# A hybrid attention layer on one core: fox scores and values as two free streams, memory tiles loaded ahead, decode preparation in four steps

## Chip, cores and metric

The program runs on one core of a Trainium2 chip. The metric is the device time of one execution in microseconds (us). TensorE (PE) does the matmuls and transposes, VectorE (DVE), ScalarE (ACT) and GpSimd (POOL) the rest; SyncE (SP) issues every DMA.

## The reference, cut to what matters

One layer over a prompt of 2048 tokens (D 1024) and 8 decode streams of 16 tokens with caches of 2048. A projection of the normalised input feeds three branches: forgetting attention ("fox", 8 heads of 64), retention (4 heads), and cross-attention to 256 memory tokens (4 heads of 128). Each is gated, projected, merged, and goes through one output projection. The change concerns fox and memory attention:

```python
def fox_attend(q, c_q, q_pos, k, v, c_k):
    s = jnp.einsum('bqhd,bkhd->bhqk', q, k) * (DH_FOX ** -0.5)
    s = s + c_q[..., :, None] - c_k[..., None, :]      # (axes swapped to heads first)
    s = jnp.where(k_pos[None, :] <= q_pos[:, None], s, -jnp.inf)
    p = jax.nn.softmax(s, axis=-1).astype(v.dtype)
    return jnp.einsum('bhqk,bkhd->bqhd', p, v)
...
def memory_attend(q, mk, mv):
    s = jnp.einsum('bthd,bmhd->bhtm', q, mk.astype(q.dtype), preferred_element_type=jnp.float32) * (DH_MEM ** -0.5)
    p = jax.nn.softmax(s, axis=-1).astype(q.dtype)
    return jnp.einsum('bhtm,bmhd->bthd', p, mv.astype(q.dtype))
```

For the prompt c is the running sum of log f, k_pos up to the query's own; for the decode the queries see the cached keys (with the sums of the cached log f taken from the end) and their own 16.

## The kernel before, in words

The program first runs the projection of all tokens (up to 1683 us), then a **weave** of two lanes, then out blocks 1 to 4.

- The right lane runs retention and then `fox` (L1252): 64 units (h, b), a head and a block of 256 queries. `scores(h, b)` goes through chunks of 512 keys, twice each (128 queries at a time): matmuls into a PSUM tile sc (L1290, L1291, the mask L1293; there are two sc banks), a maximum on DVE (L1297), the exponential on ACT into a tile pt (L1298). At the unit's end the factors f_nm of the softmax are worked out on DVE (L1218 to L1226) and POOL scales every pt (L1302). `values(h, b)` transposes pt (L1324), splits each transpose into a high part ph (ACT, L202) and a low part pl (DVE, L205), multiplies both with the values (L1344), and gates the result (f_ot, L1350 to L1352), which a DMA stores to `ind`.
- The left lane runs `forget`, `mem_prompt` (prompt against memory), `decode_mem` (L1576: 8 units, each loads mkt and mvt of 512 KB, copies its queries mq on POOL, L1599, from mqw, L1585, which needs the loads qms; matmuls L1604, L1621), `decode_fox` (L1369: preparation, then 32 units over cached keys dkt and values dvt), and `out_block(0, 2)` (L1650), the output projection of the first 256 tokens.
- Out blocks load `ind` (iraw), weights in pieces of 512 KB (wraw), split both (ACT L221, DVE or POOL L222), and run three matmuls a tile (L226 to L228).

The order is set in two steps. The generators yield at each step, and `weave` (L1007) always takes the lane that has used the smallest budget; `paced(g, n, total)` (L1002) charges total/n a step:

```python
    yield from paced(decode_fox(*pools(st, "left", ("dp", 1), ("dw", 2))), 47, 730)
...
    psum_more(st, "right", sc=2, ov=1)
    yield from paced(fox(f0, *pools(st, "right", ("fp", 5), ("fw", 2))), 672, 670)
```

That program order is a priority; the framework's scheduler (`tile.TileContext(nc, schedule_with_timeline_sim=True)`, in `_build`) then fixes the order of instructions on each engine. On the chip every engine, and SP's queue of DMAs, works in its fixed order; an instruction that waits holds up what is behind it. A tile of a pool with n buffers is written again only when the use n tiles back is over. A pool is opened when the pools before it on its side are closed.

Inside `fox` each unit was a weave of its own: the scores of unit u (weight: its chunks) against the values of unit u-1 (weight b + 2.5); no value step crossed a unit's border.

Of the kernel before, what the change touches and what calls it, by code (L numbers as in the profile page):

```python
# [19 lines left out]
P = 128  # L20
# [52 lines left out]
def body(ctx: ExitStack, tc: tile.TileContext, a, o, stop=99):  # L73
# [106 lines left out]
    def f32(t):  # L180
        return t.bitcast(F32)

    def dma(out, in_):
        nc.sync.dma_start(out, in_)
# [1021 lines left out]
    def chunks(n):  # L1206
        out, k = [], 0
        while n - k > 0:
            r = n - k
            w = min(r, 512)  # L1210
            out.append((k, w))
            k += w
        return out
# [44 lines left out]
    def fox(f0, fp, fw):  # L1258
        kvs = {}
        nk, nq = [1], [0]  # L1260

        def scores(h, b, st):

            r = slice(h * 64, (h + 1) * 64)
            if kvs.get("head") != h:
                kvs.clear()
                kvs["head"] = h
            for c in range(b // 2 + 1):
                if (h, c) not in kvs:
                    kvs[h, c] = fox_first.pop("k", None)  # L1270
                    if kvs[h, c] is None:
                        kvs[h, c] = load_k(fp if nk[0] % 6 else f0, h, c)
                        nk[0] += 1
            cols = slice(b * 256, (b + 1) * 256)
            qa, qb = fox_first.pop("q", None) or load_q(*((f0, 1) if nq[0] % 2 == 0 else (fw, 1)), h, b)
            nq[0] += 1
            kv = [kvs[h, c] for c in range(b // 2 + 1)]
            ncx = len(chunks((2 * b + 2) * P))
            nmx = sp.tile([P, 2, 4], F32, name="f_mx")[:, :, :ncx]
            l = sp.tile([P, 2, 4], F32, name="f_l")[:, :, :ncx]  # L1280
            f = sp.tile([P, 2, 4], F32, name="f_f")[:, :, :ncx]
            pts, parts = [[], []], []
            for ci in range(ncx):
                for j in range(2):
                    k0, w = chunks((2 * b + j + 1) * P)[ci]
                    qs = slice(j * P, (j + 1) * P)
                    sc = pss()
                    last = ci == ncx - 1
                    ka, kb, _ = kv[ci]
                    T.matmul(sc[:, :w], qa[:, qs], ka[:, :w], start=True, stop=False)  # L1290
                    T.matmul(sc[:, :w], qb[:, qs], kb[:, :w], start=False, stop=not last)  # L1291
                    if last:
                        T.matmul(sc[:, w - P:w], identb, maskb, start=False, stop=True)  # L1293
                    pt = fw.tile([P, 512], F32, name="pt", bufs=14)
                    pts[j] += [pt[:, i * P:(i + 1) * P] for i in range(w // P)]
                    parts.append((pt[:, :w], f[:, j, ci:ci + 1], j))
                    V.tensor_reduce(nmx[:, j, ci:ci + 1], sc[:, :w], AX.X, ALU.max, negate=True)  # L1297
                    S.activation(pt[:, :w], sc[:, :w], AF.Exp, bias=nmx[:, j, ci:ci + 1], accum_out=l[:, j, ci:ci + 1])  # L1298
                    yield
            r = softmax_scale(nmx, l, f, 2, ncx, "f_")  # L1300
            for pt, fb, j in parts:
                G.tensor_scalar(pt, pt, fb, 0.5 if r is None else r[:, j:j + 1], ALU.mult, ALU.mult)  # L1302
            st += [pts, kv]

        def values(h, b, st):

            pts, kv = st
            r = slice(h * 64, (h + 1) * 64)
            base = 64 * (h % 2)
            cols = slice(b * 256, (b + 1) * 256)  # L1310
            fg = fw.tile([P, 256], F32, name="fg")
            dma(fg[base:base + 64], fgd[r, cols])
            ov = pso()

            def prep(k2):
                p = ptp()
                pv = p.rearrange("p (k t) -> p k t", k=2)
                ph = fw.tile([P, 2, 256], F32R, name="ph", bufs=5)
                pl = fw.tile([P, 2, 256], F32R, name="pl", bufs=5)
                for kk in range(2):  # L1320
                    for j in range(2):
                        if k2 == b and kk == 1 and j == 0:
                            continue
                        T.transpose(pv[:, kk, j * P:(j + 1) * P], pts[j][2 * k2 + kk], ident)  # L1324
                if k2 == b:
                    split(ph[:, 0], pl[:, 0], pv[:, 0])
                    split(ph[:, 1, P:], pl[:, 1, P:], pv[:, 1, P:])
                else:
                    split(ph, pl, pv)
                return ph, pl  # L1330

            ahead = [prep(0)]
            yield
            if b:
                ahead.append(prep(1))
            for k2 in range(b + 1):
                parts = ahead.pop(0)
                if k2 + 2 <= b:
                    ahead.append(prep(k2 + 2))
                for i, part in enumerate(parts):  # L1340
                    for kk in range(2):
                        kt = 2 * k2 + kk
                        q0 = P if k2 == b and kk == 1 else 0
                        T.matmul(ov[:, q0:256], kv[kt // 4][2][:, kt % 4], part[:, kk, q0:],  # L1344
                                 start=kt == 0 and i == 0, stop=kt == 2 * b + 1 and i == 1)
                yield
            ot = fw.tile([P, 256], F32, name="f_ot")
            bs = slice(base, base + 64)
            os = slice(64 - base, 128 - base)
            S.copy(ot[bs], ov[os, :256])  # L1350
            V.tensor_tensor(ot[bs], ov[bs, :256], ot[bs], ALU.add)
            G.tensor_tensor(ot[bs], ot[bs], fg[bs], ALU.mult)  # L1352
            dma(ind[r, cols], ot[bs])

        units = [(h, b) for h in range(4) for b in range(8)] + [(h, 0) for h in range(4, 8)] + [(h, b) for h in range(4, 8) for b in range(1, 8)]
        prev = None
        for h, b in units:
            st = []
            gens = [(scores(h, b, st), 2 * len(chunks((2 * b + 2) * P)) + 1)]
            if prev is not None:  # L1360
                gens.append((values(*prev), prev[1] + 2.5))
            yield from weave(*gens)
            if prev is not None:
                fox_done.add(prev[:2])
            prev = (h, b, st)
        yield from values(*prev)


    def decode_fox(dp, dw):  # L1369
# [17 lines left out]
            V.tensor_tensor(lc[:, :, j], lc[:, :, j], lc[:, :, j + 1], ALU.add)  # L1387
        tot = dp.tile([P, NB, 8], F32, name="ctot")
        V.tensor_copy(tot, lc[:, :, 0])

        tp = dp.tile([P, P], F32, name="sufm")
        p = pdt()
# [3 lines left out]
        T.matmul(p[:, :64], tp, tot.rearrange("p b h -> p (b h)"), start=True, stop=True)  # L1396
        suf = dp.tile([P, NB, 8], F32, name="csuf")
        V.tensor_copy(suf, p[:, :64].rearrange("p (b h) -> p b h", b=NB))

        p = pdt()  # L1400
        T.matmul(p[:, :8], kc[:, K_BLK:K_BLK + P], lfs, start=True, stop=True)
# [2 lines left out]
        cnr = dp.tile([P, 2, 8], F32R, name="cnr")  # L1404
        V.tensor_copy(cnr[:, 0], cn)
        V.tensor_tensor(cnr[:, 1], cn, f32(cnr)[:, 0], ALU.subtract)
        p = pdt(F32R)
        T.transpose(p[:16, :P], cnr.rearrange("p a h -> p (a h)"), identr)
        cnT = dp.tile([16, P], F32R, name="cnT")
        V.tensor_copy(cnT, f32(p)[:16, :P])  # L1410

        ln = dp.tile([16, NB, 8], F32, name="ln")
        dma(ln, lfd.rearrange("(b t) h -> t b h", t=TS))
# [159 lines left out]
        yield from wave([unit(b, h) for b in range(8) for h in range(4)])  # L1573


    def decode_mem(dp, dw):  # L1576
        sl0 = slice(SAMPLE * P, (SAMPLE + 1) * P)
        mg = dp.tile([P, 4, P], F32, name="mmg")
        dma(mg, mgd[:, sl0].rearrange("(g p) t -> p g t", p=P))
# [11 lines left out]

        def unit(b):
            bs = slice(b * TS, (b + 1) * TS)
            kt = dw.tile([P, 4, 256], F32, name="mkt")
            vt = dw.tile([P, 2, 512], F32, name="mvt", bufs=4)
            dma(kt, a["cache_mem_k"][b].rearrange("h p m -> p h m"))
            dma(vt, a["cache_mem_v"][b].rearrange("(m p) c -> p m c", p=P))
            z = qblk[b % 2]
            G.tensor_copy(z[:, :, 0:TS], qw[:, :, bs])  # L1599
            qb = z.rearrange("p h c -> p (h c)")[:, :256].rearrange("p (h c) -> p h c", h=4)  # L1600
# [96 lines left out]
    with ExitStack() as st3:  # L1697
        wout = []

        def lane_left():  # L1700
            with ExitStack() as st:
                psum_more(st, "left", ys=2)
                with ExitStack() as s2:
                    yield from paced(forget(*pools(s2, "left", ("fg", 1))), 3, 17)
                with ExitStack() as s2:
                    yield from paced(mem_prompt(*pools(s2, "left", ("dp", 1), ("dw", 2))), 35, 160)
                with ExitStack() as s2:
                    yield from paced(decode_mem(*pools(s2, "left", ("dp", 1), ("dw", 2))), 13, 100)
            with ExitStack() as st:
                psum_more(st, "left", ys=1, ym=1)  # L1710
                yield from paced(decode_fox(*pools(st, "left", ("dp", 1), ("dw", 2))), 47, 730)
            while not {(h, 0) for h in range(8)} <= fox_done:
                yield 5
            psum_more(st3, "left", mm=2)
# [73 lines left out]
```

## Time and profile before

| | before |
|---|---|
| median of 3 runs | 3237.03 us (3231.66 to 3248.15) |
| the profiled execution | 3236.31 us, span 3234.5 us |
| mean granted clock of TensorE | 0.974 |
| busy: PE, DVE, ACT, POOL | 3061.6, 2034.8, 1605.4, 826.4 us |
| DMA | 660.80 MB, mean 204 GB/s |

Times count from the span's start. An engine is busy from an instruction's start to its end; a PE instruction's end is modelled, so that matmuls that follow one another overlap, and the distance from start to start tells the rate. The clock is the share of full TensorE speed (2.4 GHz) that was granted. A wait is put down to the instruction or DMA that came last.

### The profile page before, as it was taken

To read this page: it belongs to the slowest core of one execution; us is meant where nothing else is said; L and a number is where in the kernel's file an instruction comes from. 1 tells how busy PE (TensorE), PEld (TensorE's weight loads), DVE (VectorE), ACT (ScalarE), POOL (GpSimd) and SP (SyncE) were. 2 spreads that over 40 slices of the span, in tenths; PEclk is the share of its full clock that TensorE was granted. 3 is DMA by queue.
4 is the path that set the end of the run, shared out by engine and by line. 5 is a ranking of instruction groups with operands and counts; after the bars stand their busy time and mean duration, and the time that the engine had idled before them with its cause. 6 is when DMAs were issued, how large, how long until landed. Compare 5 with 4: busy or idle time off the path is not lost.

```text
span 3234.5 us, 58278 instructions
## 1 busy us (share of the span) xinstructions
PE 3061.6 (95%) x21731; PEld 2813.4 (87%) x21731; DVE 2034.8 (63%) x3390; ACT 1605.4 (50%) x3201; POOL 826.4 (26%) x789
## 2 busy tenths in 40 slices
PE   5999899999999999999988987999999998999999
PEld 5999899999999999999987984677767787889799
DVE  7776666765465565656556763776767785554544
ACT  4544354545445455545534653676777863222222
POOL 4455534211121010021001121444444462000100
PEclk8999999999999999999998998899999999999999
DMA  4766565667666657766657888566676467666665
GB/s 159 245 221 224 189 200 180 200 216 221 201 199 194 188 185 238 250 189 208 210 199 240 260 273 225 178 217 182 185 231 196 116 172 242 199 192 203 183 199 160
DMA packets 638447, 660.80 MB, mean 204 GB/s; under 512 B 46060, under 2 KB 553348, under 8 KB 638100
## 3 DMA queue, kind: packets, MB, share of 16 engines
q1 hardware_dynamic: 638164, 657.08, 65.8%
q8 instruction: 172, 2.82, 0.4%
q14 instruction: 111, 0.91, 0.1%
HBM read 477.52 MB, written 179.41 MB: 203 GB/s over the span
## 4 chain that ended last, share of the span: by engine, by line
PE 70%; DMA 12%; DVE 8%; ACT 3%; issue 3%; POOL 2%; SPq 1%; DVEq 0%; ACTq 0%; POOLq 0%
PE a L449 7%; PE a L451 7%; PE a L450 7%; PE b L449 5%; PE b L451 5%; PE b L450 5%; PE ov L1344 3%; PE tp L1324 3%; PE sc L1290 2%; DMA out_y_p<-x 2%; DVE wl L400 2%; DMA x<-in_x_prompt 2%; PE tp L226 1%; PE tp L227 1%; PE tp L228 1%
## 5 line engine op out<-in xcount | busy, mean ns | idle before, releaser
L400 DVE TENSOR_TENSOR wl<-wr,wh 128x1024 fp32r<-128x1024 f32 (+1 forms) x386 | 562.4, 1461 | 291.2 <-ACT wh L399 285.9
L399 ACT CAST wh<-wr 128x1024 fp32r<-128x1024 f32 (+1 forms) x386 | 404.7, 1050 | 308.9 <-PE b L451 129.0
L449 PE MATMUL a<-wh,ho 128*128 128x256 f32 (+1 forms) x1432 | 407.2, 285 | 15.6 <-ACT gz L707 8.8
L450 PE MATMUL a<-wl,ho 128*128 128x256 f32 (+1 forms) x1432 | 405.3, 283 | 5.8 <-DVE wl L400 5.8
L451 PE MATMUL a<-wh,ho 128*128 128x256 f32 (+1 forms) x1432 | 405.8, 284 | 1.1 <-DVE ho L276 1.1
L449 PE MATMUL b<-wh,ho 128*128 128x256 f32 (+1 forms) x1032 | 291.7, 283 | 5.3 <-DVE raw L510 2.2
L451 PE MATMUL b<-wh,ho 128*128 128x256 f32 (+1 forms) x1032 | 291.1, 283 | 5.4 <-DVE ho L276 5.4
L221 ACT CAST wh<-wraw 128x1024 fp32r<-128x1024 f32 x120 | 123.1, 1049 | 339.9 <-DMA wraw<-in_w_p 143.7
L450 PE MATMUL b<-wl,ho 128*128 128x256 f32 (+1 forms) x1032 | 291.0, 282 | 0.3 <-DVE wl L400 0.3
L449 PEld LDWEIGHTS a<-wh,ho 128*128 128x128 f32 x1432 | 272.3, 190 | 19.4 <-ACT gz L707 10.9
L450 PEld LDWEIGHTS a<-wl,ho 128*128 128x128 f32 x1432 | 272.6, 190 | 6.3 <-DVE wl L400 6.3
L451 PEld LDWEIGHTS a<-wh,ho 128*128 128x128 f32 x1432 | 272.6, 190 | 1.5 <-DVE ho L276 1.5
L428 POOL TENSOR_TENSOR wr<-wr 128x1024 f32<-128x1024 f32 (+1 forms) x72 | 200.7, 2788 | 272.7 <-DMA wr<-in_w_in 213.0
L449 PE MATMUL a<-ho,wh 128*128 128x384 f32 (+1 forms) x768 | 252.5, 329 | 1.7 <-ACT gz L707 1.7
L450 PE MATMUL a<-ho,wh 128*128 128x384 f32 (+1 forms) x768 | 252.9, 329 | 0.0
L451 PE MATMUL a<-ho,wl 128*128 128x384 f32 (+1 forms) x768 | 252.1, 329 | 0.0
L1302 POOL TENSOR_SCALAR pt<-pt,f_f,f_nm 128x512 f32<-128x512 f32 (+3 forms) x288 | 210.1, 749 | 163.1 <-DVE f_nm L1226 96.9
L460 ACT COPY kp<-a 128x256 f32<-128x256 f32 (+3 forms) x384 | 153.2, 404 | 182.9 <-PE a L451 182.4
L1298 ACT ACTIVATE pt<-sc,f_mx 128x512 f32<-128x512 f32 (+2 forms) x320 | 200.5, 628 | 66.5 <-DVE f_mx L1297 47.4
L205 DVE TENSOR_TENSOR pl<-tp,ph 128x512 fp32r<-128x512 f32 (+2 forms) x352 | 193.7, 561 | 60.6 <-ACT ph L202 58.5
L1297 DVE TENSOR_REDUCE f_mx<-sc 128x1 f32<-128x512 f32 (+2 forms) x320 | 191.6, 604 | 54.8 <-PE sc L1291 26.3
L449 PEld LDWEIGHTS b<-wh,ho 128*128 128x128 f32 x1032 | 195.6, 190 | 6.4 <-DVE raw L510 2.8
(367 smaller groups left out, 8262.8 us busy)
## 6 DMA issues: line engine op xcount, KB each, us to landing
wr<-in_w_in SPq DMA_DIRECT2D x170, 512.0 KB
wraw<-in_w_p SPq DMA_DIRECT2D x80, 512.0 KB
dkt<-in_cache_fox_k SPq DMA_DIRECT2D x64, 512.0 KB
dvt<-in_cache_fox_v SPq DMA_DIRECT2D x64, 512.0 KB
wr<-sum_gl SPq DMA_DIRECT2D x48, 512.0 KB
wraw<-in_w_out SPq DMA_DIRECT2D x40, 512.0 KB
gtd<-gz SPq DMA_DIRECT2D x96, 192.0 KB
gt<-gtd SPq DMA_DIRECT2D x24, 768.0 KB
```

Of the source, the lines that this page charges most:

```text
L205: V.tensor_tensor(l, src, f32(h), ALU.subtract)
L221: S.copy(whv[:, i * hc:(i + 1) * hc], rv)
L399: S.copy(h, t)
L400: eng.tensor_tensor(l, t, f32(h), ALU.subtract)
L428: G.tensor_tensor(out, x, y, op)
L449: T.matmul(out, lh(c), rh(c), start=first and c == 0, stop=False, skip_group_check=True)
L450: T.matmul(out, lh(c), rl(c), start=False, stop=False, skip_group_check=True)
L451: T.matmul(out, ll(c), rh(c), start=False, stop=last and c == 3, skip_group_check=True)
L460: S.copy(t[nm], t["a"])
L1297: V.tensor_reduce(nmx[:, j, ci:ci + 1], sc[:, :w], AX.X, ALU.max, negate=True)
L1298: S.activation(pt[:, :w], sc[:, :w], AF.Exp, bias=nmx[:, j, ci:ci + 1], accum_out=l[:, j, ci:ci + 1])
L1302: G.tensor_scalar(pt, pt, fb, 0.5 if r is None else r[:, j:j + 1], ALU.mult, ALU.mult)
```

## The change

1. `fox` is driven by two streams that go on across units: `score_steps`, one chunk a step, and `value_steps`. A value step comes only when its place plus the work of its unit plus LEAD = 3 is not beyond the place of the scores: values run a whole unit and three score steps behind. pt gets 17 buffers instead of 14. `fox_done` is set by the value stream.
2. The memory tiles get a pool `ml` of their own (mkt 2, mvt 3 buffers; before 2 and 4 in dw), opened ahead of `mem_prompt`; units 0 and 1 are loaded at its steps 15 and 20.
3. `decode_fox` yields four times inside its preparation; its pace is 51 steps for the budget of 730 instead of 47.

```diff
-                    pt = fw.tile([P, 512], F32, name="pt", bufs=14)
+                    pt = fw.tile([P, 512], F32, name="pt", bufs=17)
...
-        prev = None
-        for h, b in units:
-            st = []
-            gens = [(scores(h, b, st), 2 * len(chunks((2 * b + 2) * P)) + 1)]
-            if prev is not None:
-                gens.append((values(*prev), prev[1] + 2.5))
-            yield from weave(*gens)
-            if prev is not None:
-                fox_done.add(prev[:2])
-            prev = (h, b, st)
-        yield from values(*prev)
+        LEAD = 3
+        work = [2 * len(chunks((2 * b + 2) * P)) for h, b in units]
+        ready, spos = [], 0.0
+        def score_steps():
+            for u, (h, b) in enumerate(units):
+                st = []
+                for _ in scores(h, b, st):
+                    yield 1
+                ready.append(st)
+        def value_steps():
+            base = 0.0
+            for u, (h, b) in enumerate(units):
+                for n, _ in enumerate(values(h, b, ready[u])):
+                    yield base + work[u] * (n + 1) / (b + 2)
+                base += work[u]
+                fox_done.add((h, b))
+        vs, vpos, ends = value_steps(), 0.0, [sum(work[:u + 1]) for u in range(len(units))]
+        for _ in score_steps():
+            spos += 1
+            yield
+            while True:
+                u = next(i for i, e in enumerate(ends) if vpos < e - 1e-6)
+                if len(ready) <= u or vpos + work[u] + LEAD > spos:
+                    break
+                vpos = next(vs)
+                yield
+        for _ in vs:
+            yield
...
     def decode_fox(dp, dw):
         V.tensor_copy(tot, lc[:, :, 0])
+        yield
...
         V.tensor_copy(suf, p[:, :64].rearrange("p (b h) -> p b h", b=NB))
+        yield
...
         V.tensor_tensor(cnr[:, 1], cn, f32(cnr)[:, 0], ALU.subtract)
+        yield
...
         V.tensor_copy(cnT, f32(p)[:16, :P])
+        yield
...
-    def decode_mem(dp, dw):
+    def mem_load(ml, b):
+        kt = ml.tile([P, 4, 256], F32, name="mkt", bufs=2)
+        vt = ml.tile([P, 2, 512], F32, name="mvt", bufs=3)
+        dma(kt, a["cache_mem_k"][b].rearrange("h p m -> p h m"))
+        dma(vt, a["cache_mem_v"][b].rearrange("(m p) c -> p m c", p=P))
+        return kt, vt
+
+    def decode_mem(ml, first, dp, dw):
...
+            kt, vt = first.pop(b, None) or mem_load(ml, b)
...
+                    for n, step in enumerate(paced(mem_prompt(*pools(s2, "left", ("dp", 1), ("dw", 2))), 35, 160)):
+                        if n in (15, 20):
+                            first[len(first)] = mem_load(ml, len(first))
+                        yield step
...
-                yield from paced(decode_fox(*pools(st, "left", ("dp", 1), ("dw", 2))), 47, 730)
+                yield from paced(decode_fox(*pools(st, "left", ("dp", 1), ("dw", 2))), 51, 730)
```

How the order moves is shown at three places, first before and then now.

**SP, the memory tiles.** Before, the loads of mkt and mvt stand behind everything of the prompt's memory work (qms are the decode's queries, m_ot a result of the prompt's part):

```order
L184 DMA qms0_21335<-mqH_92 128x4x128
L184 DMA qms1_21336<-mqL_93 128x4x128
L184 DMA qb_21897<-crq_81 4x256
L184 DMA mkt_21365<-in_cache_mem_k 128x4x256
L184 DMA mvt_21366<-in_cache_mem_v 128x2x512
L184 DMA mkt_21396<-in_cache_mem_k 128x4x256
L184 DMA mvt_21397<-in_cache_mem_v 128x2x512
L184 DMA mvt_21434<-in_cache_mem_v 128x2x512
```

Now the first five stand right behind the loads of the prompt's own memory keys and values (mkT, mvf), ahead of its query loads mqh and mql:

```order
L184 DMA mkT0_18527<-mkH_94 128x4x256
L184 DMA mkT1_18528<-mkL_95 128x4x256
L184 DMA mvf_18533<-mvd_96 128x2x512
L184 DMA mkt_19946<-in_cache_mem_k 128x4x256
L184 DMA rv_19117<-rvd_87 128x1024
L184 DMA mvt_19947<-in_cache_mem_v 128x2x512
L184 DMA mkt_20429<-in_cache_mem_k 128x4x256
L184 DMA mvt_20430<-in_cache_mem_v 128x2x512
L184 DMA mvt_21437<-in_cache_mem_v 128x2x512
L184 DMA kb_21463<-crk_82 4x512
L184 DMA mqh_18770<-mqH_92 128x256
```

Five loads have moved up by some 240 places; the loads qms have not moved.

**PE, the preparation of the fox decode.** L1396 (L1419 in the changed kernel) is the first matmul on ctot. Before, five score chunks follow one another ahead of it, and the next steps of the preparation follow it; the last three chunks and these steps:

```order
L1290 MATMUL sc_22464<-ka_21888,qa_22378 128x512
L1291 MATMUL sc_22464<-kb_21889,qb_22379 128x512
L1290 MATMUL sc_22484<-ka_22249,qa_22378 128x384
L1291 MATMUL sc_22484<-kb_22250,qb_22379 128x384
L1293 LDWEIGHTS identb_66
L1293 MATMUL sc_22484<-maskb_68,identb_66 128x128
L1290 MATMUL sc_22495<-ka_22249,qa_22378 128x512
L1291 MATMUL sc_22495<-kb_22250,qb_22379 128x512
L1293 LDWEIGHTS identb_66
L1293 MATMUL sc_22495<-maskb_68,identb_66 128x128
L1396 MATMUL tp_22148<-ctot_22142,sufm_22144 128x64
L1401 MATMUL tp_22152<-lfs_98,kc_64 128x8
```

Now the first transpose (L1416) and that matmul stand between the score and value matmuls of fox:

```order
L1416 MATMUL tp_22386<-kc_64 128x128
L1344 MATMUL ov_22306<-ph_22352,vv_21852 128x256 x2
L1344 MATMUL ov_22306<-pl_22353,vv_21852 128x256 x2
L1344 MATMUL ov_22306<-ph_22372,vv_22077 128x256
L1290 MATMUL sc_22466<-ka_21850,qa_22414 128x512
L1291 MATMUL sc_22466<-kb_21851,qb_22415 128x512
L1344 MATMUL ov_22306<-ph_22372,vv_22077 128x128
L1344 MATMUL ov_22306<-pl_22373,vv_22077 128x256
L1344 MATMUL ov_22306<-pl_22373,vv_22077 128x128
L1290 MATMUL sc_22494<-ka_22075,qa_22414 128x512
L1291 MATMUL sc_22494<-kb_22076,qb_22415 128x512
L1419 MATMUL tp_22389<-ctot_22228,sufm_22385 128x64
```

The next steps of the preparation (L1425, L1433) follow 43 and 100 rows later, each among fox's work.

**PE, the tail.** dos is the last result of a decode unit, mm a sum of out block 0. Before, the decode's last transpose is at row 14879, and out block 0 begins at 14925, between fox's scores and values, which go on to 15467:

```order
L1344 MATMUL ov_31037<-ph_31082,vv_30813 128x256
L226 MATMUL mm_31261<-ih_31213,wh_31249 128x256
L227 MATMUL mm_31261<-il_31214,wh_31249 128x256
L1290 MATMUL sc_31361<-ka_31008,qa_31141 128x384
L1291 MATMUL sc_31361<-kb_31009,qb_31142 128x384
L1293 LDWEIGHTS identb_66
L1293 MATMUL sc_31361<-maskb_68,identb_66 128x128
```

Now fox's last matmul (ov) is row 15122, the decode's last follow it, and out block 0 comes after both:

```order
L1525 MATMUL ym_31453<-dvt_31702,dpr_31696 32x128 x8
L1525 MATMUL ym_31453<-dvt_31712,dpr_31696 32x128 x8
L1533 MATMUL ym_31453<-dvw_31728,dpr_31723 32x128 x4
L1539 MATMUL tp_31736<-kc_64,dos_31734 128x128
L226 MATMUL mm_31805<-ih_31757,wh_31793 128x256
L227 MATMUL mm_31805<-il_31758,wh_31793 128x256
```

Out block 0 has no fox matmuls left beside it; the decode's have moved to the end of fox. On SP the loads of out block 1 (iraw 128x2x512, 512 KB) now stand among the first of block 0 (iraw 128x2x256, wraw); before, there was none of block 1 at this place:

```order
L184 DMA iraw<-ind 128x2x256
L184 DMA x<-in_x_prompt 128x256
L184 DMA iraw<-ind 128x2x512 x2
L184 DMA wraw<-in_w_p 128x8x128 x2
L184 DMA iraw<-ind 128x2x256 x2
L184 DMA iraw<-ind 128x2x512 x2
L184 DMA wraw<-in_w_p 128x8x128
L184 DMA iraw<-ind 128x2x256 x2
L184 DMA wraw<-in_w_p 128x8x128
L184 DMA iraw<-ind 128x2x512 x2
L184 DMA wraw<-in_w_p 128x8x128
L184 DMA iraw<-ind 128x2x256 x2
```

The last of block 0's eight iraw loads comes after five of its wraw and six of block 1's iraw.

## Rows read from the trace of the kernel before

**Rows 1.** Windows: stretch, length, busy us (count) by engine, clock, DMA share, GB/s.

```profile
1683.00:1987.00 304.00, 266.01 (x1566) 225.30 (x1566) 187.81 (x535) 150.28 (x368) 46.62 (x121) 0.92 0.85 261
1987.00:2680.00 693.00, 640.62 (x5165) 502.86 (x5165) 498.23 (x1181) 494.89 (x1357) 331.21 (x457) 0.95 0.62 183
```

**Rows 2.** Waits of PE, 1987 to 2680: total us, times, longest us.

```profile
PE sc L1290 <- ACT pt L1298: 22.0, 37, 2.0
PE tp L1324 <- POOL pt L1302: 8.8, 5, 5.5
PE tp L1396 <- DVE ctot L1389: 4.5, 1, 4.5
```

**Rows 3.** Timeline of PE: start, us, instruction, idle before and its releaser.

```profile
1729.67 0.36 PE L226 MATMUL ys<-mkT,mqh 128*128 128x256 f32 x1 [1.94 <-DMA mqh<-mqH]
...
1943.50 6.45 PE L1604 MATMUL ys<-mkt,mq 128*64 128x256 f32 x16 [9.17 <-DMA mkt<-in_cache_mem_k]
...
1957.32 1.91 PE L1604 MATMUL ys<-mkt,mq 128*64 128x256 f32 x8 [1.78 <-DMA mkt<-in_cache_mem_k]
...
1970.99 6.36 PE L1604 MATMUL ys<-mkt,mq 128*64 128x256 f32 x16 [4.03 <-DMA mkt<-in_cache_mem_k]
```

**Rows 4.** Timeline of all engines, 1940 to 1944.

```profile
1941.98 0.69 DVE L1585 TENSOR_TENSOR mqw<-qms,qms 128x512 f32<-128x512 f32 x1 [4.82 <-DMA qms<-mqL]
1942.81 0.41 POOL L1599 COPY mq<-mqw 128x64 f32<-128x64 f32 x2 [7.75 <-DVE mqw L1585]
```

**Rows 5.** Windows at the memory tiles' new and old place.

```profile
1720.00:1730.00 10.00, 6.90 (x35) 5.24 (x33) 5.63 (x24) 2.42 (x4) 0.00 (x0) 1.00 0.98 334
1940.00:1987.00 47.00, 35.92 (x128) 17.08 (x128) 9.96 (x45) 9.95 (x32) 1.83 (x8) 0.83 0.91 253
```

**Rows 6.** Timeline of DVE and PE, the decode's preparation.

```profile
2023.78 2.55 DVE L1387 TENSOR_TENSOR lc<-lc 128x64 f32<-128x64 f32 x10
...
2026.61 0.69 PE L1396 MATMUL tp<-ctot,sufm 128*128 128x64 f32 x2 [4.46 <-DVE ctot L1389]
```

**Rows 7.** Windows of 10 us around the preparation, and the fox stage behind.

```profile
2010.00:2020.00 10.00, 6.38 (x20) 3.47 (x20) 6.31 (x16) 5.02 (x18) 3.77 (x7) 0.70 1.13 320
2020.00:2030.00 10.00, 3.61 (x16) 2.68 (x17) 7.76 (x38) 1.24 (x4) 3.07 (x6) 0.50 0.89 262
2030.00:2040.00 10.00, 10.00 (x47) 5.02 (x46) 4.89 (x16) 5.49 (x12) 0.42 (x1) 0.50 0.48 147
2040.00:2580.00 540.00, 507.87 (x4268) 392.99 (x4267) 383.31 (x917) 402.76 (x1135) 252.97 (x375) 0.96 0.63 187
```

**Rows 8.** Timeline of PE: starts of work that runs back to back.

```profile
2583.74 1.07 PE L1324 MATMUL tp<-kc,pt 128*128 128x128 f32 x8 [0.47 <-DVE pl L205]
2584.57 0.36 PE L1290 MATMUL sc<-ka,qa 128*128 128x256 f32 x1
...
2585.25 0.40 PE L1291 MATMUL sc<-kb,qb 68*128 68x512 f32 x1
2585.49 0.40 PE L1344 MATMUL ov<-ph,vv 128*128 128x256 f32 x2
2585.72 0.40 PE L1344 MATMUL ov<-pl,vv 128*128 128x256 f32 x2
```

**Rows 9.** Timeline of PE: the decode's last transpose, out block 0's first matmul.

```profile
2582.73 0.30 PE L1513 MATMUL tp<-kc,dos 128*128 128x128 f32 x1
...
2594.38 0.28 PE L226 MATMUL mm<-ih,wh 128*128 128x256 f32 x1
```

**Rows 10.** Chain of waits: start, us, what.

```profile
2587.38 5.25 DMA wraw<-in_w_p
```

**Rows 11.** Windows at the end of fox and behind it.

```profile
2580.00:2680.00 100.00, 92.86 (x717) 86.61 (x718) 80.91 (x149) 64.67 (x145) 62.71 (x57) 0.98 0.56 161
2680.00:2720.00 40.00, 33.23 (x214) 31.46 (x214) 21.30 (x25) 18.23 (x18) 7.34 (x4) 0.88 0.93 296
```

More of the change, by code (lines that the diff above doesn't have):

```diff
@@ L1593, in unit @@
             bs = slice(b * TS, (b + 1) * TS)
[L1594 to L1597, printed above, removed]
+            kt, vt = first.pop(b, None) or mem_load(ml, b)
             z = qblk[b % 2]
@@ L1704, in lane_left @@
                     yield from paced(forget(*pools(s2, "left", ("fg", 1))), 3, 17)
+                ml, = pools(st, "left", ("ml", 1))
+                first = {}
                 with ExitStack() as s2:
-                    yield from paced(mem_prompt(*pools(s2, "left", ("dp", 1), ("dw", 2))), 35, 160)
+                    for n, step in enumerate(paced(mem_prompt(*pools(s2, "left", ("dp", 1), ("dw", 2))), 35, 160)):
+                        if n in (15, 20):
+                            first[len(first)] = mem_load(ml, len(first))
+                        yield step
                 with ExitStack() as s2:
-                    yield from paced(decode_mem(*pools(s2, "left", ("dp", 1), ("dw", 2))), 13, 100)
+                    yield from paced(decode_mem(ml, first, *pools(s2, "left", ("dp", 1), ("dw", 2))), 13, 100)
             with ExitStack() as st:
                 psum_more(st, "left", ys=1, ym=1)
-                yield from paced(decode_fox(*pools(st, "left", ("dp", 1), ("dw", 2))), 47, 730)
+                yield from paced(decode_fox(*pools(st, "left", ("dp", 1), ("dw", 2))), 51, 730)
             while not {(h, 0) for h in range(8)} <= fox_done:
```

## Prediction

> **What bounds the kernel now.** I read first the windows by stage, then the waits of TensorE, then the timeline at its longest waits. The profiled execution took 3236.3 us (span 3234.5), 0.7 us under the median of 3237.0, so a sum made against the one serves for the other. In a windows row PE's busy time stands after the stretch and its length, and near the end stand PE's clock, DMA's busy share and GB/s. The projection (up to 1683 us) and the out blocks behind 2720 are touched by no line of the diff. Between them lie the retention, memory and fox stages, where PE does 266.0 of 304 us at a clock of 0.92 and then 640.6 of 693 us at 0.95 (VectorE 498.2, ScalarE 494.9) [rows 1]. PE is the bound there, and what can be won is its idle time and its low clock. The waits are many short ones: 22.0 us in 37 places where a score matmul waits until ScalarE has read the bank before, 8.8 us where a transpose waits for POOL's scaling of pt, 4.5 us for one sum on VectorE [rows 2]. A loss below is length minus busy time x clock.
>
> **Part one, memory tiles ahead.** Before, the decode side loads mkt and mvt only when the prompt's memory work is over, and PE stands 9.17, 1.78 and 4.03 us before its matmuls on mkt [rows 3]. The 9.17 will hardly shrink: the same matmul also needs the query copy mq, which POOL makes 0.7 us before, and that waits for the sum mqw, which waits for qms [rows 4]. The diff leaves qms where it was, so I take 0 to 0.5 us off this wait. The other two, 5.8 us, are loads of later units: there are still two mkt buffers, so these loads cannot start earlier. They can only land sooner, because 2.5 MB (two mkt, three mvt of 512 KB) have left a stretch in which DMA moved 253 GB/s at a share of 0.91: at that rate 9.9 us of transfer [rows 5]. Gain: 0 to 8 (those 5.8 and some low clock), estimate 5. But the order listing shows the five loads right behind mkT and mvf and ahead of all mqh and mql: they now run about 1722 us, where DMA moves 334 GB/s at a share of 0.98 [rows 5]. There they take 2.5 MB / 334 = 7.5 us, and mqh, for which PE already waits 1.94 us [rows 3], comes later by as much. Cost: 0 to 8, estimate 5. Sum of part one 0, ends -8 and +8.
>
> **Part two, preparation of the fox decode in steps.** Before, five score chunks run down back to back and PE then waits 4.46 us for ctot, which comes after ten of fifteen additions in a row on VectorE (2.55 us) [rows 6]. The stretch 2010 to 2040 holds 6.38, 3.61 and 10.0 us of PE time at clocks of 0.70, 0.50 and 0.50: 11.3 us of full-speed work in 30, a loss of 18.7 [rows 7]. The half clock (1.2 GHz) outlives the idle time: the last ten microseconds are full and still at 0.50. If only the 4.5 us wait went and the clock stayed, the gain would be 4.5. In the changed order the four stages lie fox transposes, value and score matmuls apart, so both the wait and the clock should recover. What stays is the ordinary loss of the fox stage, (540 - 507.87 x 0.96)/540 = 0.097 per us [rows 7], 2.9 in 30 us, and some of the burst of cache loads behind it. Ends 0 and -15.8; I take -14, near the far end, since the run of bunched scores is gone.
>
> **Part three, the two streams.** The same instructions are issued and the total of steps stays 672; only their order and three more pt buffers change. An upper end for the gain is all of the score and POOL waits, 22.0 + 8.8 = 30.8 us [rows 2]. For a cost I priced the PE work that stands, in the order of each kernel, between a score chunk and the one two places before it (it needs that bank): a transpose 0.10 us (eight in 0.83), a half of a 512-wide score 0.24, a 256-wide matmul 0.12 [rows 8]. Counting how far these spaces fall short of 1.5 us gives 21.7 us before, close to the 22.0 that were waited. It gives 32.6 us after, 11 more (over 316 spaces instead of 276; for the same number, 7 more). So the order shows no gain in this wait; the deeper buffers should win a part of the 8.8. Ends -31 and +11. I take 0: the count is the nearer evidence, and it and the POOL wait cancel.
>
> **Part four, the tail.** The decode now takes 51 steps of 14.3 instead of 47 of 15.5, and with the streams it ends with the last fox values. Before, it ended at 2582.7 and out block 0 began at 2594.4, 11.7 us later, beside fox [rows 9]. After, the first matmul of out block 0 stands behind the last of fox and of the decode. By the prices of [rows 8] the fox and decode work before 2582.7 is 448 us if every matmul follows at its own rate; from 1983 it took 600, less the loss of part two 581: a ratio of 1.30. Fox's share behind it is 30 us. Before, these 30 us and out block 0 (576 matmuls at 0.12 us, 68 to 69) took from 2583 to about 2712, 129 us. After: 30 x 1.30 = 39, a gap, and 68. The gap is at least the 11.7 shown. SP's order now has the iraw loads of the next out block among those of block 0: about 7.5 MB before the last piece that block 0's first column needs, 25 us at the 296 GB/s of 2680 to 2720 [rows 11]. With 4.7 us until the first wraw is issued (2582.7 to 2587.4 [rows 9, 10]) and some matmuls done meanwhile, the upper end is 26 us. I take 20, nearer the upper: 39 + 20 + 68 = 127, -2 against before, ends -10 and +4. The loads of block 1 are then paid for, so what is lost before block 1 (10.8 us lost in 2680 to 2720 [rows 11]) are part of this -2.
>
> **Sum.** 0 - 14 + 0 - 2 = -16 us: 3236.3 - 16 = 3220 us.
>
> **The rivals.** A: the order wins nothing lasting. The preparation's gain is halved (-7) because PE, which works in order, now meets the four stages one by one, each with a short wait for VectorE, and part one and the bunched scores cost 4: -3, 3233 us. For it: the waits of [rows 2] are short and many, the kind that come back elsewhere; against it: the 0.50 clock of [rows 7] is one place with one cause.
> B, the other side: out block 0 loses its cover. Before, its matmuls fill fox's idle places; now fox runs alone to its end and out block 0 alone behind it. This decides if the ratio of 1.30 rises with the spacing of part three: at 1.35 the 478 us of fox and decode cost 24 us more, with the gap at 26 the tail another 6, and with part two halved 7 more: -16 + 37 = +21, 3257 us. It turns slower from a ratio of about 1.335 on. For it: the count of 32.6; against it: the pt buffers. The Trainium skill (Perfetto Trace Analysis, "Optimization Strategy") says that stages with different limits gain by being interleaved; this change takes such a mixture apart at the tail, and by that rule this rival would come true. The trace bears some of it out: the mixed 2580 to 2680 lost 9.0 us in 100 [rows 11], little less than the 0.097 per us of the fox stage with the decode in it, so the cover is worth about a microsecond by the windows and 10 (30 x 0.30) by the bare work.
> C: the streams do what they are built for. A whole unit and three steps between scores and values hide POOL's scaling and ScalarE's reads, 24 of the 30.8 us go, and the short low clocks with them (loss in 2040 to 2580: 52.4 [rows 7]): -16 - 25 = 3195 us. For it: VectorE's and ScalarE's busy times are below PE's. Against it: the bunched scores.
>
> **Chances.** Forecast 0.38 (3205 to 3230), A 0.24, B 0.2, C 0.18. A measurement of this kernel can tell some 0.5%, 16 us, from no change: faster means below 3221, slower above 3253. The forecast's own range straddles that line, about half below; with nearly all of C and a little of A that gives faster 0.45, slower 0.15 (most of B's upper half and unforeseen waits), the same 0.40. The range reaches to C below and B above, from the bounds of parts two to four: 3186 to 3254.
>
> **What would show it.** Right: PE's wait for ctot under 2 us and the clock above 0.8 in every ten microseconds of the preparation; the score waits on ScalarE still 20 us or more; the first wait for mkt still above 8 us; between the last fox value matmul and the first of out block 0 some 11 us of idle PE, and no 10 us of gaps before block 1. Wrong: a score wait under 10 us (C), a fox stage without the preparation above 1.33 of its bare work (B), or a new wait of over 10 us on mqh about 1725.

## The result, and the profile after

The changed kernel takes 3267.6 us (median of 4 runs, 3264.0 to 3273.0); before took 3237.3 in the same comparison. The ratio is 1.0083 (95% interval 1.0057 to 1.0108): **slower by 27 us** by the ratio (the medians are 30 apart), where 16 us faster was forecast and 3186 to 3254 us given as the range. The profiled execution took 3273.0 us (span 3271.1), 36.7 more than the profiled one of before.

The tail comes first, since it is there that the time went. Windows of the changed kernel, columns as in [rows 1]:

```profile
2040.00:2580.00 540.00, 503.34 (x4099) 388.85 (x4097) 394.35 (x947) 404.29 (x1143) 251.94 (x375) 0.96 0.61 182
2580.00:2640.00 60.00, 45.46 (x453) 37.41 (x451) 33.30 (x71) 34.89 (x87) 22.78 (x33) 0.90 0.47 146
2640.00:2680.00 40.00, 27.79 (x168) 25.54 (x169) 27.43 (x34) 19.22 (x24) 12.30 (x7) 0.72 0.83 257
2680.00:2760.00 80.00, 68.73 (x476) 63.44 (x476) 42.66 (x50) 24.00 (x27) 25.09 (x15) 0.98 0.69 206
```

The same windows of the kernel before (the first is in [rows 7]):

```profile
2580.00:2640.00 60.00, 55.86 (x414) 50.58 (x415) 52.50 (x103) 46.22 (x112) 40.80 (x38) 0.97 0.62 176
2640.00:2680.00 40.00, 37.00 (x305) 36.03 (x305) 28.41 (x48) 18.45 (x33) 21.91 (x19) 1.00 0.48 140
2680.00:2760.00 80.00, 73.22 (x385) 63.64 (x385) 40.26 (x49) 26.66 (x28) 12.52 (x8) 0.94 0.82 253
```

Length minus busy time x clock, summed over the last three windows, is 19.1 + 20.0 + 12.6 = 51.7 us after against 5.8 + 3.0 + 11.2 = 20.0 before: 31.7 us of loss more, nearly all between 2620 and 2680, where the clock fell to 0.72 on the mean of 40 us. PE's timeline there:

```profile
2629.41 0.47 PE L1539 MATMUL tp<-kc,dos 128*128 128x128 f32 x1 [0.37 <-ACT dos L1535]
2642.22 0.58 PE L226 MATMUL mm<-ih,wh 128*128 128x256 f32 x1 [12.34 <-ACT wh L221]
...
2659.43 0.79 PE L226 MATMUL mm<-ih,wh 128*128 128x256 f32 x2 [4.63 <-ACT ih L202]
...
2696.29 0.39 PE L228 MATMUL mm<-ih,wl 128*128 128x256 f32 x1 [1.65 <-POOL wl L222]
...
2703.88 0.39 PE L228 MATMUL mm<-ih,wl 128*128 128x256 f32 x1 [1.58 <-POOL wl L222]
```

The decode's last transpose (L1539) is followed by 12.3 us of idle PE, then out block 0 starts at half clock (2640 to 2660 at 0.50), waits again for late pieces of its input (ih), and from 2696 on, at full clock, it waits in every column for POOL's part of the weights (wl). What answers to the rows of the other parts:

```profile
1736.05 0.77 PE L226 MATMUL ys<-mkT,mqh 128*128 128x256 f32 x2 [5.98 <-DMA mkT<-mkH]
...
1747.97 0.55 PE L226 MATMUL ys<-mkT,mqh 128*128 128x256 f32 x1 [4.09 <-DMA mqh<-mqH]
...
1948.48 5.70 PE L1634 MATMUL ys<-mkt,mq 128*64 128x256 f32 x16 [8.62 <-POOL mq L1629]
...
1959.22 1.91 PE L1634 MATMUL ys<-mkt,mq 128*64 128x256 f32 x8 [0.45 <-DMA mkt<-in_cache_mem_k]
...
1965.81 3.18 PE L1634 MATMUL ys<-mkt,mq 128*64 128x256 f32 x8 [2.15 <-DMA mkt<-in_cache_mem_k]
...
2036.62 0.41 PE L1419 MATMUL tp<-ctot,sufm 128*128 128x64 f32 x2
```

PE now waits 5.98 us for mkT and 4.09 for mqh, where [rows 3] had 1.94 for mqh. The tiles do not stand ahead of all mqh, as the order was read: three of these loads are issued from 1695 to 1705, and the one waited for is the fourth, behind the tiles. The load of mkT stands ahead of the tiles; it was itself issued 10.7 us later than before, and SP's last wait ahead of it is for a store of `forget` (crk<-rc). SP's timeline, mkT before, then three rows and a wait of now:

```profile
1720.58 0.37 SPq L184 DMA_DIRECT2D mkT<-mkH  x1
...
1705.13 0.43 SPq L184 DMA_DIRECT2D mqh<-mqH  x1
...
1731.32 0.37 SPq L184 DMA_DIRECT2D mkT<-mkH  x1
...
1739.53 0.34 SPq L184 DMA_DIRECT2D mqh<-mqH  x1
SPq L184 <- DMA crk<-rc: 2.2, 1, 2.2
```

Windows of the two stretches, the first two of before, the others of now:

```profile
1683.00:1760.00 77.00, 58.24 (x308) 49.37 (x309) 48.70 (x123) 32.46 (x76) 6.69 (x15) 0.82 0.85 272
1900.00:1983.00 83.00, 63.77 (x316) 43.66 (x314) 34.48 (x108) 26.66 (x70) 13.08 (x42) 0.88 0.95 281
1683.00:1760.00 77.00, 52.24 (x286) 43.39 (x285) 46.26 (x113) 31.47 (x70) 7.82 (x14) 0.82 0.94 301
1900.00:1983.00 83.00, 69.01 (x358) 48.77 (x356) 38.13 (x118) 30.20 (x80) 16.42 (x49) 0.92 0.86 264
```

The loss goes from 29.2 to 34.2 us in the first stretch and from 26.9 to 19.5 in the second. The first wait of the memory decode is still 8.62 us and is now put down to mq; the later ones fell from 1.78 and 4.03 to 0.45 and 2.15. The wait for ctot is gone. The preparation's 30 us:

```profile
2010.00:2020.00 10.00, 6.94 (x40) 4.84 (x39) 6.35 (x14) 5.82 (x18) 4.53 (x9) 1.00 0.90 238
2020.00:2030.00 10.00, 8.34 (x29) 6.32 (x30) 9.14 (x27) 5.76 (x16) 4.67 (x7) 0.55 0.95 335
2030.00:2040.00 10.00, 9.43 (x62) 7.97 (x61) 9.50 (x27) 7.43 (x20) 5.57 (x7) 0.94 0.38 119
```

Their loss is 3.1 + 5.4 + 1.1 = 9.6 us instead of the 18.7 of [rows 7]; one window of low clock is left. PE's waits in the fox stage, 1987 to 2620:

```profile
PE sc L1290 <- ACT pt L1298: 21.6, 42, 1.3
PE sc L1290 <- DMA qa<-qtL: 5.2, 4, 1.7
...
PE tp L1324 <- POOL pt L1302: 1.3, 5, 0.3
```

The score waits on ScalarE did not move (22.0 in [rows 2]); the transposes' wait for POOL went from 8.8 to 1.3, and the wait for the query loads qa is 5.2, where it was 1.1 before.

### The profile page after: what moved, and what is told of

Its sections match the earlier page's. It is cut to its first block, busy times and chain, and to the rows that moved or that the text cites. A ratio compares the mean times of both kernels' runs of the same rounds, so it can differ in the third digit from the quotient of the medians.

```text
span 3271.1 us, 58224 instructions
## 1 busy us (share of the span) xinstructions
PE 3069.9 (94%) x21731; PEld 2820.4 (86%) x21731; DVE 2050.4 (63%) x3390; ACT 1606.9 (49%) x3201; POOL 820.2 (25%) x789
## 5 line engine op out<-in xcount | busy, mean ns | idle before, releaser
L1302 POOL TENSOR_SCALAR pt<-pt,f_f,f_nm 128x512 f32<-128x512 f32 (+3 forms) x288 | 202.6, 718 | 201.3 <-DVE f_nm L1226 82.4
```

## The experiments

**What the pace was.** The diff keeps `paced(fox(...), 672, 670)`, and ahead of the result I took the steps to be 672 in both kernels. They are not. `weave` (L1007) yields once more for each generator that ends, so the old fox, a weave per unit, yields 672 + 127 = 799 times, each charged 670/672: a budget of 797. The new fox yields 672 times: 670. In units of budget the old fox ended at 1042 (245 for the retention and 797), behind the decode (988, that is 17 + 155 + 100 + 716 for the steps of its lane), and out block 0 opened at 988, with fox still going on. The new fox ends at 915, 73 ahead of the decode, and out block 0 opens when fox has closed. This gave the first four runs, made on one chip, with three theories of where the time went: T (the tail), S (the streams), M (the memory tiles).

`e1_pace_797`, the changed kernel with the old pace:

```diff
-                    pt = fw.tile([P, 512], F32, name="pt", bufs=17)
+                    pt = fw.tile([P, 512], F32, name="pt", bufs=14)
...
-                yield from paced(fox(...), 672, 670)
+                yield from paced(fox(...), 672, 797)
```

> The changed kernel with fox's pace set back: the old fox yielded 799 times against its nominal 672, so its budget came to 797 and it ended behind the decode; the new one yields exactly 672 times, budget 670, and ends before it. Here 672 steps cost 797 again, and pt has 14 buffers (with 15 or more the pools of out block 0 do not fit beside fox). In its order out block 0 begins among fox's last scores again. Theory T (the tail: out block 0 lost its fox cover): 3210 to 3235 us. Theory S (the two streams themselves run slower, bunched scores): 3250 us or more, with the gap before out block 0 gone. Theory M (the memory tiles at 1722 us cost it): 3250 or more with 8 us more loss before 1760.

Measured 3236.8 us, 0.9979 (0.9966 to 0.9993) of before: 1.04% under the changed kernel, 34 us. (All ratios are to runs of before on the same chip, and differences between kernels go by them.) T: out block 0 has fox beside it again and the loss is gone, though 2 us over T's range in us (before itself took 3242.7 on that chip).

```profile
2040.00:2580.00 540.00, 502.25 (x4254) 384.61 (x4254) 382.18 (x920) 399.09 (x1126) 250.73 (x369) 0.96 0.62 188
2580.00:2640.00 60.00, 54.03 (x386) 48.07 (x385) 50.14 (x96) 42.41 (x101) 35.17 (x35) 0.97 0.61 168
2640.00:2680.00 40.00, 38.17 (x317) 37.22 (x316) 27.74 (x49) 20.68 (x38) 24.63 (x21) 1.00 0.56 161
2680.00:2760.00 80.00, 73.65 (x395) 64.00 (x395) 42.62 (x52) 28.57 (x30) 13.69 (x9) 0.96 0.82 249
```

In these windows of e1 the tail loses 7.6 + 1.8 + 9.3 = 18.7 us instead of 51.7: 33 us less, which is about all that separates the two kernels. The first window loses as much as in the changed kernel (57.8 against 56.8).

`e2_before_fast_fox`, the kernel before with the new pace alone (`672, 670` becomes `799, 670`):

> The kernel before with fox's pace alone changed: its 799 yields now share a budget of 670, so fox ends before the decode and, in the order, out block 0 has no fox beside it; streams, memory tiles and preparation are as before. T: 3255 to 3280 us, an idle stretch of over 10 us before out block 0. S and M: within 8 us of 3237.

Measured 3276.5 us, 1.0099 (1.0083 to 1.0116). With streams, tiles and preparation as before, the pace alone gives the whole slowdown and more. PE's timeline and the windows of the tail in e2:

```profile
2649.43 0.58 PE L226 MATMUL mm<-ih,wh 128*128 128x256 f32 x1 [11.97 <-ACT wh L221]
...
2666.67 0.80 PE L226 MATMUL mm<-ih,wh 128*128 128x256 f32 x2 [4.63 <-ACT ih L202]
```

```profile
2580.00:2640.00 60.00, 53.79 (x512) 44.63 (x511) 41.63 (x93) 42.19 (x114) 30.34 (x43) 0.99 0.30 93
2640.00:2680.00 40.00, 20.46 (x112) 18.82 (x113) 26.98 (x29) 19.95 (x24) 10.21 (x5) 0.62 0.95 292
2680.00:2760.00 80.00, 68.56 (x501) 64.42 (x500) 38.74 (x51) 24.06 (x27) 25.79 (x15) 0.98 0.67 197
```

The same idle 12 us, the same 4.63 us for ih, a clock of 0.62 behind: 46.8 us lost, 26.8 more than before.

`e3_rest_only`, the changed kernel without streams (the old fox with pt 14, at its budget of 797; tiles ahead and preparation in steps stay):

> The changed kernel without the two streams (fox as before, pt 14): memory tiles ahead and the four steps of the preparation stay; out block 0 begins among fox's last scores, as before. T: 3220 to 3237 us (the preparation's loss of 18.7 falls by 8 to 14, the tiles cost 0 to 5). S: the same. M: 3245 or more.

Measured 3224.2 us, 0.9937 (0.9916 to 0.9957). T and S both hold, M falls. It is faster than both kernels. Against it e1 says what the streams cost where out block 0 has its cover: 0.9979 - 0.9937 = 0.42%, 13.6 us, give or take some 8 by the two intervals. Both have 14 pt buffers; the streams with the 17 of the change were not run with cover. The windows of e3 put the cost in the fox stage:

```profile
2040.00:2580.00 540.00, 512.76 (x4335) 395.98 (x4333) 396.67 (x947) 408.16 (x1149) 256.44 (x379) 0.97 0.63 190
```

The loss is 42.6 us in these 540, in e1 57.8. (The two profiled executions differ by only 4.4 us, since e1's lost some 10 us less in the first 400 us, which no edit touches: 51.5 against 61.2.)

`e4_mem_only`, the kernel before with the tiles ahead alone:

> The kernel before with the memory tiles ahead alone. Program order and paces are as before, but in the scheduled order the decode is drawn out to fox's end and out block 0 begins only behind both, as in the changed kernel. T: 3255 to 3280 us although no stream was touched. S: 3230 to 3240. M: 3240 to 3250, lost before 1760, with a short gap at the tail.

Measured 3238.2 us, 0.9985 (0.9970 to 0.9999). The premise of this expectation is false: on the chip out block 0 begins at 2590.9, and fox's last value matmul is at 2670.8, as before. So the run says nothing on T. It prices the tiles alone: -0.15%, 5 us, just clear of noise, and M falls.

The next four, on one chip again. `e5_yields_only`, the kernel before with the four `yield` in `decode_fox` and `51, 730`:

> The kernel before with the four steps of the decode's preparation alone (51 steps of the budget of 730). Theory P (the forecast's part two, gains add up): the ratio of e3 to e4 is 0.995, so this alone gives 0.993 to 0.997 of before, with the wait for ctot gone. Theory Q (the gain of e3 comes from the tiles and the steps together): 0.998 to 1.002.

Measured 3227.5 us, 0.9957 (0.9944 to 0.9971): 14 us less, so P holds. Tiles and steps (-0.15% and -0.43%) add up to about e3 (-0.63%).

`e6_after_wl_dve`, the changed kernel with the weight parts of out block 0 on VectorE (`wout[0], po, po, pw, G` becomes `..., None`):

> The changed kernel, but out block 0 makes the second half of each low weight part (wl) on VectorE instead of POOL. In the changed kernel a column of out block 0 takes 7.4 us where its 48 matmuls need 5.8, and the last thing waited for is POOL's wl (2.4 us each, VectorE 1.3). Theory F (without fox beside it out block 0 is held up by its own weight chain): 8 to 12 us less than the changed kernel, 3255 to 3261 us, columns of 6 us. Theory G (the loss is all in the start: idle time, late iraw loads, half clock): within 3 us of 3267.

Measured 3263.2 us, 1.0078 (1.0055 to 1.0101): 0.05% or 2 us under the changed kernel, far inside the intervals: inconclusive by the time. In its trace POOL's waits for wl in the tail are gone and others came (6.1 us for gm, 8.1 instead of 5.5 for ih); the matmuls of out block 0 begin within 98.7 us of one another, in the changed kernel within 102.7. That makes the weight chain worth some 4 of the 33 us in these two executions.

`e7_rest_d680`, e3 with the decode's budget at 680 (`51, 730` becomes `51, 680`):

> e3 with the decode's budget at 680 instead of 730: it ends earlier, and out block 0 begins with 36 of fox's score chunks still to come instead of 20. In e3 out block 0 still ran some 38 us alone behind fox. Theory T (cover is worth time): 3 to 10 us less than e3, 3214 to 3221 beside an e3 of 3224. Rival D (the decode, pressed together, costs fox what the tail gains): within 3 us of e3, or slower.

Measured 3250.0 us, 1.0031 (1.0015 to 1.0046), 0.94% more than e3: T in its plain form is wrong. Out block 0 began at 2569.7, 136 us ahead of fox's end, and ended with it. Then it was block 1 that had nothing beside its loads:

```profile
2715.62 1.22 PE L226 MATMUL mm<-ih,wh 128*128 128x512 f32 x2 [9.28 <-ACT ih L202]
...
2724.66 0.72 PE L226 MATMUL mr<-ih,wh 128*128 128x512 f32 x2 [1.28 <-ACT ih L202]
...
PE sc L1290 <- DMA qa<-qtL: 11.2, 7, 3.0
PE mm L226 <- ACT ih L202: 10.0, 2, 9.3
```

10.0 us went at block 1's start, where no wait of e3 reaches 1.5. More went in the fox stage: 2040 to 2580 loses 61.3 us, 18.7 more than in e3, and PE waits 11.2 us there for qa.

`e8_e1_qfirst`, e1 with the query loads ahead:

```diff
+            qa, qb = fox_first.pop("q", None) or load_q(...)
             if kvs.get("head") != h:
...
-            qa, qb = fox_first.pop("q", None) or load_q(...)
```

> e1 with the loads of qa and qb written ahead of the key loads of the same unit. e1 was 0.42% slower than e3 (the streams' own cost) and PE waited 14.4 us for qa there, up to 6.9 at a head's change, where SP issued five key tiles' loads first; in e3 it waited 4.1. Theory K (the streams cost by these late query loads): 5 to 12 us less than e1 and a wait on qa below 6 us. Rival: the cost is spread over the fox stage (bunched scores): within 3 us of e1.

Measured 3240.0 us, 0.9994 (0.9979 to 1.0008); e1 had 0.9979. The wait for qa in 2040 to 2580 fell from 14.4 to 7.2 us and the time did not: K falls. In the same stretch the score waits on ScalarE rose from 9.9 to 15.1 us, so most of it came back there.

The last four asked whether the effects add and which part of the tail costs. `e9_rest_fast`, e3 with `799, 670`:

> e3 (tiles and steps, fox as before) with fox's 799 yields paced to 670, so that out block 0 again stands behind fox and decode: the changed kernel without its two streams. Theory T (pace costs about 1.0%, as from before to e2 and from e1 to the changed kernel; effects add): 1.003 to 1.007 of before, 3248 to 3260 us; the changed kernel (1.0083) is then 0.2 to 0.5% above it, which is the streams' own cost. Rival (the streams cost nothing when out block 0 has no cover anyway): 1.008 to 1.010.

Measured 3271.9 us, 1.0094 (1.0063 to 1.0125). The rival holds, though the interval touches T's upper end: without cover the streams cost nothing that can be seen (the changed kernel 1.0083), and the 0.63% that tiles and steps won in e3 are gone too (e2, without them, 1.0099). The effects do not add across the tail.

`e10_rest_d760`, e3 with `51, 760`:

> e3 with the decode's budget at 760: out block 0 begins with 4 of fox's score chunks to come instead of 20, still before fox's last value matmuls, so its first weights land while PE has fox to do, but more of it runs alone. Theory H (what costs is the idle start and the half clock behind it, not the lack of cover as such): within 5 us of e3, 0.992 to 0.996. Theory T in its plain form (every microsecond of cover is worth 0.3): 5 to 12 us more than e3, 0.996 to 0.999.

Measured 3248.3 us, 1.0019 (1.0002 to 1.0037): 0.82% over e3, 27 us, above both. No idle start is left (no wait of PE over 3 us from 2560 to 2760), yet the time is lost: H in its strict form falls, and plain T said 5 to 12 us. But the tail is not where most of it went: 2580 to 2760 loses 21.8 us (e3 15.0), while 2050 to 2550 loses 54.8 (e3 39.4). There PE waits longer for the decode's cached keys (dkt) and for qa, first e3 and then e10:

```profile
PE ys L1467 <- DMA dkt<-in_cache_fox_k: 2.1, 4, 0.9
PE sc L1290 <- DMA qa<-qtL: 4.1, 2, 2.9
PE ys L1467 <- DMA dkt<-in_cache_fox_k: 11.3, 5, 5.0
PE sc L1290 <- DMA qa<-qtL: 8.8, 4, 5.0
```

These two waits are 13.9 us longer, most of the 15.4. So this run, too, cannot price the cover by itself.

`e11_e1_lead0`, e1 with `LEAD = 0`:

> e1 (both streams, pace 797) with LEAD 0: the values follow a unit behind, without the three further score steps. Theory L (the lag holds buffers of queries, keys and pt longer, and that is the streams' cost of 0.4%): 0.994 to 0.9965 of before. Rival (the even interleave itself, bunched scores, costs it): within 0.1% of e1, 0.997 to 0.999.

Measured 3239.2 us, 0.9998 (0.9984 to 1.0012): no gain over e1 (0.9979), L falls.

`e12_after_d656`, the changed kernel with `51, 656`:

> The changed kernel with the decode's budget at 656, so that in program order it ends with fox instead of 73 budget units behind it, and out block 0 opens at once; in the order the first matmul of out block 0 stands 53 rows ahead of fox's last value matmul. Theory H: the idle start shrinks, 5 to 20 us less than the changed kernel, 1.002 to 1.0065. Plain T: out block 0 is still alone for nearly all its length, within 5 us of 3267, 1.007 to 1.010.

Measured 3251.5 us, 1.0029 (1.0013 to 1.0044): 0.54% or 17 us under the changed kernel, H's range. Its first out-block matmul is 13 us ahead of fox's last, and the 12 us wait for the first weights is gone; an idle stretch of 8.4 us at 2641, put down to gm on VectorE, is left:

```profile
2641.30 0.55 PE L226 MATMUL mm<-ih,wh 128*128 128x256 f32 x1 [8.38 <-DVE gm L1702]
...
2640.00:2680.00 40.00, 33.21 (x249) 32.49 (x250) 28.10 (x39) 18.97 (x22) 16.12 (x9) 0.92 0.90 275
```

All by the overlap, that is the time from the first matmul of out block 0 to fox's last value matmul in the profiled execution:

| kernel | overlap, us | ratio to before |
|---|---|---|
| e9, e2, after, e6 | -18, -14, -19, -19 | 1.0094, 1.0099, 1.0083, 1.0078 |
| e12 | 13 | 1.0029 |
| e10 | 39 | 1.0019 |
| e8, e1, e11 | 67, 68, 70 | 0.9994, 0.9979, 0.9998 |
| before, e5, e4, e3 | 77, 77, 80, 79 | 1, 0.9957, 0.9985, 0.9937 |
| e7 | 136 | 1.0031 |

With the old streams and with the new, the ratio goes with the overlap: the kernels without any lie at 1.008 to 1.010, those with 13 to 39 us at 1.002 to 1.003, those with 67 to 80 at 1.000 or under, and the one with 136 at 1.003 again. The decode's budget, which moves the overlap in e7, e10 and e12, also changes how dense the decode stands in fox, and in e7 and e10 most of the loss lies there. Nearest to the overlap alone are the pairs in which only the pace moved: from before to e2 the three windows of the tail lose 26.8 us more, from e3 to e9 40.0 (55.0 against 15.0).

## Why the prediction was wrong

The step that failed is part four. It took the tail at -2 us, where the lost cover of out block 0 costs some 34 (e1 against the changed kernel); part three, put at 0, was 14 off. By its own steps:

- **Part one** (sum 0, ends -8 and +8): right in size, partly by luck. By the windows above the cost is 5 us and the gain 7, where 5 and 5 were taken; the first wait stayed, and e4 measured -5. But the cost was to be mqh's alone, behind the tiles. The larger wait is mkT's, which SP issues ahead of them, 10.7 us later than before; in e4, with the tiles alone, it is issued at 1730.5 too, in e5, without them, at 1722.2. So the tiles did delay the prompt's memory work, but not in the way that was forecast.
- **Part two** (-14): right in place and size, e5 measured -14. In the changed kernel the stretch itself won 9.1 us; that the clock would recover at once was too much, 2020 to 2030 still shows 0.55. And it is a gain of a kernel with cover: without cover, tiles and steps together win nothing that can be seen (e9 1.0094, e2 1.0099).
- **Part three** (0, ends -31 and +11): its first sentence is false. "The total of steps stays 672" is true of the number in the call, not of what the old fox yielded; the diff had a pace change in it that I took for a constant. The streams themselves, at equal pace and 14 pt buffers, cost 14 us (e1 against e3), just beyond the upper end. The wait for the score banks, forecast to grow by 11, did not (21.6 against 22.0); the 1.5 us by which the spaces were counted stands in no row. The waits for qa are only part of the 14, since e8 halved them for nothing. Lag (e11) is not it either. What costs these 14 us stays open.
- **Part four** (-2, ends -10 and +4): the term that was mis-sized. It saw the right order (out block 0 behind fox and decode) and the right start (12.3 us of idle, 11.7 taken as the least). It put the end of the decode at 1983 + 478 x 1.30 = 2604; it came at 2629. And it gave the gap 20 us: from 2629.4 to out block 0's last matmul at 2744.7 are 115 us, 47 more than its 68. 25 + 27 = 52 us, which is the way from -16 to the +36.7 of the profiled execution. The 25 are not the streams': in e9, with the old fox, the decode's last transpose stands at 2631.4. Left out of the gap were the half clock behind the idle start, the further waits for ih, and the 7 to 7.6 us a column with POOL's wl (from 2696.29 to 2703.88 in the timeline above).

One part after the other, by ratios: tiles and steps -0.63% (e3), streams +0.42% (e1), pace +1.04% (the changed kernel): +0.83%, 27 us. The sum comes out by construction, and the shares depend on the order: with the pace taken second (e9) it is +1.57%, and the streams behind it -0.11%. Rival B was what came: its mechanism (out block 0 loses its cover), and nearly its ratio (636.8/478 = 1.33, the stretch from 1983 to 2629.4 less the 9.6 of the preparation), with a gap of 47 where it had 26. It had 0.2, and its 3257 us lay beyond the range that was said to reach to it. That out block 0 loses its cover had been read in the order; what was missing was its price, and the pace only says why the order moved. The place named there, the Trainium skill's "Optimization Strategy" (Perfetto Trace Analysis), says no more than that interleaving stages with different most-contended engines may improve performance. The table agrees with it up to 80 us of overlap. In e7, with 136, block 1 had to start without cover (10.0 us of waits).

That the pace alone costs 32 to 34 us is shown, by e1 and e2, each of which changes it in one of the two kernels (e1 also takes pt back to 14); from e3 to e9 it costs 1.57%, 51 us. The division of the changed kernel's loss is read from its windows of 20 us:

```profile
2620.00:2640.00 20.00, 7.32 (x126) 4.96 (x124) 4.08 (x9) 5.93 (x11) 0.73 (x1) 0.71 0.79 241
2640.00:2660.00 20.00, 10.09 (x38) 8.62 (x39) 14.46 (x15) 11.91 (x15) 6.37 (x3) 0.50 0.99 306
2660.00:2680.00 20.00, 17.70 (x132) 16.92 (x131) 12.97 (x20) 7.30 (x10) 5.93 (x4) 0.93 0.68 209
```

Idle time is 12.7 + 9.9 + 2.3 = 24.9 us, low clock (busy time x what is missing to 1) 2.1 + 5.0 + 1.2 = 8.3. Behind 2680 the tail loses little more than before (12.6 against 11.2). Three things stay open: what in the even interleave of the streams costs 14 us with cover and nothing without it; why the gain of tiles and steps is gone without cover; and why a decode spread further (e10) waits longer for its loads. Loading block 0's weights under fox with 17 pt buffers was not tried: its pools do not fit beside fox.

## What to carry to other kernels

Where generators share a pace, count what they yield before and after a change, not the number in the call: a rewrite that drops 127 empty steps is a change of order everywhere behind. Price a stage that loses its neighbour by what the neighbour hid (here the first loads and the clock after the idle start, less so a slow engine's share of the weights), not by its matmuls and one gap. Keep the two parts that won here, the preparation in steps (14 us) and the tiles ahead (5, barely clear of noise), and leave the old fox: e3, 0.63% under before.

## What was not expected of the hardware

That the clock falls to half at a place where so much work is waiting. In the 20 us from 2640 to 2660 (row above) PE was busy half of the time, with DMA at a share of 0.99 and 306 GB/s, and the clock stayed at 0.50 through all of it, after the 12.3 us of idle PE: 10.1 us busy gave, by busy time x clock, 5.0 us of full-speed work. In e12, with 13 us of overlap, the loss in 2640 to 2680 is 9.4 us at a clock of 0.92 (row at e12) instead of 20.0 at 0.72.
